# Later splits and later accumulations of the last product's weights in the gate stage of a transformer trunk kernel

## Chip, cores and metric

The kernel runs on one core of one Trainium2 chip. The metric is the device time of one execution in microseconds (us); a kernel's time is the median of its runs.

## The reference

One layer, in float32, of a trunk with sliding-window attention and a gated embedding (512 tokens, width 2048). Cut to what matters:

```python
hn = rmsnorm(x, norm_g)
y = swa_mixer(hn, swa_w_in, swa_w_out, swa_sinks, rel_bias)   # attention, times silu(gate), then @ w_out
x = x + y
emb = p @ ple_proj                                  # 512x256 @ 256x2048
g = jax.nn.sigmoid(rmsnorm(x, ple_norm) @ ple_gate) # 512x2048 @ 2048x2048
x = x + emb * g
return rmsnorm(x, final_g)
```

The change touches the product with `ple_gate`, which is called the gate stage here.

## The kernel before

**Precision.** Every product of two float32 matrices is made of three matmuls (`mm3`, lines 126 to 128). An operand is split into a high part (the value cast to fp32r, on ACT) and a low part (the value minus the high part, on DVE), and high x high, low x high and high x low are accumulated in PSUM. For the weights of the last two stages `_split` does this: line 754 is the cast (`bhi`), line 755 the subtraction (`blo`).

**Fewer products.** The 2048x2048 products with `w_out` and `ple_gate` are computed by blocks in Strassen's manner, with seven block products. Six of them are run one after the other in the order `ORDER_PLE = (1, 7, 6, 5, 3, 4)`; the remaining one, numbered 2, is broken up once more into small products that are spread over products 1, 7 and 6. Counted with it, the code's `p == 5` is the fifth product, `p == 3` the sixth and `p == 4` the last, and so they are called here.

**Pieces.** The weights come in pieces of 128x1024 (512 KB). `Pieces.specs` lists them in the order of use. A product has eight pieces, four for each half `jj`; between them stand pieces for the small products (half the matmuls) and for the embedding (`ple_proj`, the tile `e` in PSUM). A whole piece feeds 12 matmuls. `B.get(i)` hands out piece `i`. Before that it calls `ahead(i)`, which issues loads some pieces ahead (line 747, on SP's queue, into `braw`, whose buffers are reused in turn) and has the splits of pieces up to `i + 2` made.

**Grown pieces.** Products 7, 6 and 4 use weights that are sums of blocks, each being the one before plus one more block. So product 7's eight pieces are loaded into tiles called `grown` ("seed"), and POOL issues accumulating DMAs (line 734, `accum_op=ALU.add`) that add the next block on top of the same tile once it has been split: once for product 6, once more for product 4. `get(i)` puts the accumulation for the next product on the list `due` at position `i + 2` (behind a seed) or `i + 6`; it is issued when `get` reaches that position.

**The last product's weights.** The eight pieces of product 4 are split by `split_last(k)`, ahead of time, at places that the table `early` names by product, half and step: line 762 is the cast on ACT (tile `last`), line 763 the subtraction on DVE (tile `low`). Piece 0 is split in the fifth product, pieces 1 to 6 in the sixth, piece 7 behind it. The last product then runs as four blocks (tiles `last` and `open` in PSUM), between which the rows of the result are normalised and stored.

**Posts.** When a product's sums are complete, their values are passed through `gated`: sigmoid on ACT (line 1224), times the embedding on DVE (line 1226), added to `x1`, and squared on ACT for the final norm (line 1233). For eight of the sixteen parts the addition is an accumulating DMA that POOL issues (line 1228, `x1s<-s`); for the others it is on DVE (line 1230). Line 1392 and line 1267 are steps that sum products; line 855, 867 and 868 prepare and split the other operand for the next product; line 1243 and 1251 are of the final norm.

**Order.** In the gate stage the instructions of every engine (PE, SP, DVE, ACT and POOL) run in the order in which the program issues them. So a later place in the Python program is a later place in each engine's queue, and an instruction that waits holds up those behind it on its own engine.

Of the kernel before, what the change touches and what calls it, by code (L numbers as in the profile page):

```python
# [55 lines left out]
def trunk_kernel(ctx: ExitStack, tc: tile.TileContext, a: dict):  # L56
# [31 lines left out]
    class Weights:  # L88
# [24 lines left out]
        def get(self, i):  # L113
            while self.asked <= min(i + self.ahead, len(self.srcs) - 1):
                self.todo.append(partial_of(self._make, self.asked))
                self.asked += 1
            while self.todo and not (self.apart and i < len(self.made)):
                self.todo.pop(0)()
            return self.made[i]
# [281 lines left out]
    for b in range(exact, BUCKETS):  # L401
        d = np.nonzero(bk == b)[0]
        if len(d):
            lo, n = P - 1 + int(d.min()), len(d)
# [315 lines left out]
    class Pieces:  # L720
# [37 lines left out]
        def split_last(self, k, hi, lo):  # L758

            i = len(self.specs) - 8 + k  # L760
            raw = self.base.pop(i)
            nc.scalar.copy(hi, raw)
            nc.vector.tensor_sub(lo, raw, hi.bitcast(F32))
            self.made[i] = tuple([t[:, :512], t[:, 512:]] for t in (hi, lo))
# [14 lines left out]
        def get(self, i):  # L779
            self.ahead(i)  # L780

            key = self.specs[i][2]
            if key is not None:
                n = next((n for n in range(i + 1, len(self.specs)) if self.specs[n][2] == key), None)
                if n is not None:
                    self.due.append((i + (2 if self.specs[i][0] == "seed" else 6), n))
                    self.due.sort()
            while self.due and self.due[0][0] <= i:
                self._prepare(self.due.pop(0)[1])
            return self.made.pop(i)  # L790
# [494 lines left out]


    rooms4 = {}
    early = {(5, 0, 3): 0, (3, 0, 0): 1, (3, 0, 2): 2, (3, 1, 0): 3, (3, 1, 1): 4, (3, 1, 2): 5, (3, 1, 3): 6}

    def split_last(k):  # L1290
        if k % 2 == 0:
# [108 lines left out]
        next(g)  # L1400
    for g in two:
        next(g)
    split_last(7)
    for g in two:
        run(g)
# [50 lines left out]
    n = done[3]  # L1456
# [81 lines left out]
```

## Time and profile before

| | us |
|---|---|
| median of 3 runs | 791.35 (791.12 to 792.30) |
| the profiled execution | 791.86 |
| its span | 790.1 |
| PE busy | 780.4 |
| DVE busy | 605.9 |
| ACT busy | 505.8 |
| POOL busy | 138.4 |

In the profile, times are in us from the start of the span unless marked ns. PE is the tensor engine's matmuls and PEld its weight loads, DVE the vector engine, ACT the scalar engine, POOL the GpSimd engine, SP the engine whose queue issues the plain loads and stores. A row of the timeline has the start, the busy time, engine, line, operation, tiles written `<-` read, and in brackets the idle time of the engine before it with what ended that. A row of the stretches has the stretch, its length, then each engine's busy time with its count of instructions, the granted clock of PE as a share, the DMA share (the mean busy share of 16 DMA engines, which can read a little over 1) and GB/s. A row of the waits has who waited, for whom, the total in us, how often, and the longest.

### The profile page before, as it was taken

To read this page: it belongs to the slowest core of one execution; us is meant where nothing else is said; L and a number is where in the kernel's file an instruction comes from. 1 tells how busy PE (TensorE), PEld (TensorE's weight loads), DVE (VectorE), ACT (ScalarE), POOL (GpSimd) and SP (SyncE) were. 2 spreads that over 40 slices of the span, in tenths; PEclk is the share of its full clock that TensorE was granted. 3 is DMA by queue.
4 is the path that set the end of the run, shared out by engine and by line. 5 is a ranking of instruction groups with operands and counts; after the bars stand their busy time and mean duration, and the time that the engine had idled before them with its cause. 6 is when DMAs were issued, how large, how long until landed. Compare 5 with 4: busy or idle time off the path is not lost.

```text
span 790.1 us, 11098 instructions
## 1 busy us (share of the span) xinstructions
PE 780.4 (99%) x3726; PEld 652.1 (83%) x3726; DVE 605.9 (77%) x1036; ACT 505.8 (64%) x1066; POOL 138.4 (18%) x257
## 2 busy tenths in 40 slices
PE   9999999999999999999999999999999999999995
PEld 8888888888888888888888888888888888887885
DVE  4546697876877687777777899778869588978995
ACT  6643576666767586766666645456689676556943
POOL 0201423132223323122222200000000022201000
PEclk9999999999999999999999999999999999999998
DMA  9978889999999989999997498667873899979733
GB/s 344 285 215 296 191 251 316 299 278 270 277 268 262 268 236 316 238 300 263 279 272 185 133 364 317 224 206 237 267 265 107 299 291 250 252 229 250 213 108 106
DMA packets 47561, 198.07 MB, mean 251 GB/s; under 512 B 7104, under 2 KB 8128, under 8 KB 41744
## 3 DMA queue, kind: packets, MB, share of 16 engines
q1 hardware_dynamic: 38208, 150.91, 55.1%
q0 software_dynamic: 9296, 46.46, 30.4%
q8 instruction: 29, 0.48, 0.2%
q14 instruction: 28, 0.23, 0.1%
HBM read 189.16 MB, written 71.35 MB: 330 GB/s over the span
## 4 chain that ended last, share of the span: by engine, by line
PE 93%; DVE 3%; issue 2%; ACT 1%; POOL 0%; POOLq 0%; DVEq 0%; ACTq 0%
PE gps L126 7%; PE gps L127 7%; PE gps L128 7%; PE qps L126 7%; PE qps L127 7%; PE qps L128 7%; PE o L127 6%; PE o L126 6%; PE o L128 6%; PE g L127 4%; PE g L128 4%; PE g L126 4%; PE s L485 2%; PE vps L290 2%; PE pt L551 2%
## 5 line engine op out<-in xcount | busy, mean ns | idle before, releaser
L755 DVE TENSOR_TENSOR blo<-braw,bhi 128x1024 fp32r<-128x1024 f32 x108 | 131.3, 1221 | 37.0 <-ACT bhi L754 36.2
L754 ACT CAST bhi<-braw 128x1024 fp32r<-128x1024 f32 x108 | 113.4, 1051 | 57.9 <-PE o L128 20.7
L126 PE MATMUL gps<-xh,whi 128*128 128x512 f32 x256 | 100.0, 391 | 0.0
L127 PE MATMUL gps<-xl,whi 128*128 128x512 f32 x256 | 100.0, 390 | 0.0
L128 PE MATMUL gps<-xh,wlo 128*128 128x512 f32 x256 | 99.7, 390 | 0.0
L126 PE MATMUL qps<-xh,whi 128*128 128x512 f32 x224 | 87.8, 392 | 0.0
L127 PE MATMUL qps<-xl,whi 128*128 128x512 f32 x224 | 87.4, 390 | 0.0
L128 PE MATMUL qps<-xh,wlo 128*128 128x512 f32 x224 | 87.3, 390 | 0.0
L110 DVE TENSOR_TENSOR wlo<-wraw,whi 128x1024 fp32r<-128x1024 f32 x60 | 73.5, 1226 | 3.8 <-ACT whi L109 3.7
L570 POOL TENSOR_SCALAR_AFFINE_SELECT own<-r 64x512 fp32r<-64x512 f32 (+1 forms) x48 | 32.4, 675 | 244.9 <-DVE r L560 242.4
L127 PE MATMUL o<-blo,fho 128*128 128x512 f32 x192 | 74.9, 390 | 0.0
L126 PE MATMUL o<-bhi,fho 128*128 128x512 f32 x192 | 74.9, 390 | 0.0
L128 PE MATMUL o<-bhi,flo 128*128 128x512 f32 x192 | 74.8, 389 | 0.0
L556 ACT CAST r<-pt 128x256 fp32r<-128x256 f32 x64 | 23.9, 373 | 68.5 <-PE pt L551 68.1
L109 ACT CAST whi<-wraw 128x1024 fp32r<-128x1024 f32 x60 | 62.3, 1040 | 5.4 <-issue 4.1
L127 PE MATMUL g<-blo,fhg 128*128 128x512 f32 x160 | 62.5, 391 | 0.4 <-DVE blo L755 0.4
L126 PE MATMUL g<-bhi,fhg 128*128 128x512 f32 x160 | 62.8, 392 | 0.0
L128 PE MATMUL g<-bhi,flg 128*128 128x512 f32 x160 | 62.4, 390 | 0.0
L128 PEld LDWEIGHTS gps<-xh,wlo 128*128 128x128 f32 x256 | 48.1, 188 | 10.2
L126 PEld LDWEIGHTS gps<-xh,whi 128*128 128x128 f32 x256 | 48.1, 188 | 9.2
L529 ACT ACTIVATE t<-t,sm 128x129 f32<-128x129 f32 (+1 forms) x128 | 49.7, 390 | 8.9 <-DVE sm L525 7.3
L127 PEld LDWEIGHTS gps<-xl,whi 128*128 128x128 f32 x256 | 48.1, 188 | 8.8
(240 smaller groups left out, 1762.7 us busy)
## 6 DMA issues: line engine op xcount, KB each, us to landing
wraw<-in_w_gate_in SPq DMA_DIRECT2D x32, 512.0 KB, 8.1
w_out<-in_w_out POOLq DMA_DIRECT2D x32, 512.0 KB, 8.9
braw<-w_out SPq DMA_DIRECT2D x32, 512.0 KB, 4.7
wraw<-in_w_q SPq DMA_DIRECT2D x28, 512.0 KB, 6.8
braw<-in_w_out SPq DMA_DIRECT2D x22, 512.0 KB, 4.5
braw<-in_ple_gate SPq DMA_DIRECT2D x22, 512.0 KB, 5.3
xw<-in_first SPq DMA_DIRECT2D x14, 640.5 KB, 6.6
w_out<-in_w_out SPq DMA_DIRECT2D x16, 512.0 KB, 10.8
```

The lines of the kernel that those rows point to most:

```text
L109: nc.scalar.copy(hi, raw)
L110: nc.vector.tensor_sub(lo, raw, hi.bitcast(F32))
L126: nc.tensor.matmul(ps, sh, mh, start=first, stop=False, skip_group_check=more)
L127: nc.tensor.matmul(ps, sh, ml, start=False, stop=False, skip_group_check=more)
L128: nc.tensor.matmul(ps, sl, mh, start=False, stop=last, skip_group_check=more)
L290: nc.tensor.matmul(v_ps[t], h[:, c], part_of(high_at, 256, 512), start=f, stop=e, skip_group_check=True)
L485: nc.tensor.matmul(s_ps[:, u, : 2 * n], st, of_keys[:, first * 2 * QB : (first * QB + n) * 2], start=True, stop=True)
L529: nc.scalar.activation(su, su, AF.Exp, bias=sm[:, u : u + 1], accum_out=sm[:, 2 + u : 3 + u])
L556: nc.scalar.copy(rh, src)
L570: nc.gpsimd.affine_select(out=flat(own), in_=flat(r).bitcast(F32), pattern=[[0, 8], [sign, HB]], compare_op=ALU.is_ge, fill=0.0, base=-HB ...
L754: nc.scalar.copy(hi, raw)
L755: nc.vector.tensor_sub(lo, raw, hi.bitcast(F32))
```

## The change

Three edits: an accumulation for product 4 is put on the list 14 positions behind the piece instead of 6; the table `early` no longer has an entry in product 5, and the pieces move up by one in the entries of product 3; pieces 6 and 7 are both split behind product 3, where piece 7 alone was.

```diff
@@ Pieces.get
-                    self.due.append((i + (2 if self.specs[i][0] == "seed" else 6), n))
+                    self.due.append((i + (2 if self.specs[i][0] == "seed" else 14), n))
@@ gate stage
-    early = {(5, 0, 3): 0, (3, 0, 0): 1, (3, 0, 2): 2, (3, 1, 0): 3, (3, 1, 1): 4, (3, 1, 2): 5, (3, 1, 3): 6}
+    early = {(3, 0, 0): 0, (3, 0, 2): 1, (3, 1, 0): 2, (3, 1, 1): 3, (3, 1, 2): 4, (3, 1, 3): 5}
@@
     for g in two:
         next(g)
+    split_last(6)
     split_last(7)
     for g in two:
         run(g)
```

## The prediction

> **What bounds the kernel now.** I read the page first, then the waits of PE, then the timeline around the one wait found there.
>
> ```profile
> span 790.1 us, 11098 instructions
> PE 780.4 (99%) x3726; PEld 652.1 (83%) x3726; DVE 605.9 (77%) x1036; ACT 505.8 (64%) x1066; POOL 138.4 (18%) x257
> ...
> DMA  9978889999999989999997498667873899979733
> ...
> PE 93%; DVE 3%; issue 2%; ACT 1%; POOL 0%; POOLq 0%; DVEq 0%; ACTq 0%
> ```
>
> PE is busy for 99% of the span and carries 93% of the chain that ended last, so an edit of the weight splits gains only where it ends a wait of PE, and loses only where it makes one. A digit of the DMA line is one slice of 19.75 us: in the last quarter of the span, the gate stage, most digits but the last few are 7 to 9, so the transfers are the second resource to watch. From 620 to 782 us the view of waits lists this and nothing else for PE:
>
> ```profile
> PE g L127 <- DVE blo L755: 0.4, 1, 0.4
> ```
>
> The timeline of PE places it:
>
> ```profile
> 712.34 0.39 PE L126 MATMUL g<-bhi,fhg 128*128 128x512 f32 x1
> 713.15 0.50 PE L127 MATMUL g<-blo,fhg 128*128 128x512 f32 x1 [0.42 <-DVE blo L755]
> 713.49 0.40 PE L128 MATMUL g<-bhi,flg 128*128 128x512 f32 x1
> 713.73 0.40 PE L126 MATMUL g<-bhi,fhg 128*128 128x512 f32 x1
> ```
>
> Undisturbed ones of this shape follow each other like this:
>
> ```profile
> 743.05 0.39 PE L126 MATMUL g<-bhi,fhg 128*128 128x512 f32 x1
> 743.28 0.39 PE L127 MATMUL g<-blo,fhg 128*128 128x512 f32 x1
> 743.50 0.39 PE L128 MATMUL g<-bhi,flg 128*128 128x512 f32 x1
> ```
>
> That is a step of 0.227 us. At 712 the steps are 0.81, 0.34 and 0.24: 0.58 + 0.11 + 0.01 over the pitch, and with a few more 0.24 steps behind them about **0.76 us** lost. What DVE does just before:
>
> ```profile
> 709.61 1.21 DVE L855 TENSOR_TENSOR hT<-hT,hT 128x1024 f32<-128x1024 f32 x1
> 710.74 1.22 DVE L763 TENSOR_TENSOR low<-grown,last 128x1024 fp32r<-128x1024 f32 x1
> 711.88 3.49 DVE L755 TENSOR_TENSOR blo<-braw,bhi 128x1024 fp32r<-128x1024 f32 x3
> ```
>
> L763 is the split of the last product's piece 0, the one that the change takes out of the fifth product. The split that PE waits for (first of the three at 711.88) comes right behind it.
>
> **Part 1: piece 0's split leaves the fifth product.** DVE's steps from start to start are 1.14 us (710.74 to 711.88), more than PE's stall of 0.58. Without L763 the awaited split ends 1.14 us earlier and the stall goes: **-0.76 us**. What is late next: the casts of the sixth product, below.
>
> **Part 2: one more split behind the sixth product.** All splits between move up by one piece but keep their number in each slot, so DVE and ACT there are unchanged. Behind the sixth product stand two splits where one stood: one L763 more on DVE (1.14 us) and one cast on ACT.
>
> ```profile
> 758.56 1.22 DVE L763 TENSOR_TENSOR low<-grown,last 128x1024 fp32r<-128x1024 f32 x1
> ...
> 773.17 0.69 DVE L1392 TENSOR_TENSOR s<-last,s 128x512 f32<-128x512 f32 x1 [0.90 <-PE last L128]
> ...
> 777.30 0.69 DVE L1243 TENSOR_TENSOR x1s<-x1s,fg 128x512 f32<-128x512 f32 x1 [0.79 <-ACT s L1233]
> ...
> 781.79 0.42 DVE L1226 TENSOR_TENSOR s<-e,s 128x256 f32<-128x256 f32 x1 [1.53 <-PE e L128]
> ```
>
> DVE works without a gap from 758.56 to about 772; 1.14 us more uses up the 0.90 of idle time before 773.17, leaves 0.24, and the 1.53 before 781.79 takes that. When PE needs them:
>
> ```profile
> L127 PE MATMUL last<-low,fhg x24: 389/389/390, 754.2 to 772.5; 128*128 128x512 f32 x24
> ```
>
> The first block of the last product (24 matmuls and 6 of its embedding) and pieces 4 and 5 of the second (12) take 42 x 0.227 = 9.5 us, so piece 6 is due at about 763.7, and both splits end by about 761. Cost **0**, at most 1.14 if the cover fails.
>
> **Part 3: the accumulations.** POOL issues them in program order, and nothing ties POOL to PE's pace except what each of its DMAs waits for. So "14 pieces behind" changes only their order against the other POOL DMAs, the accumulations of `gated` into x1s (L1228), which wait for DVE. By the instruction order of the changed kernel, the accumulations for pieces 0 to 2 stay ahead of all of them; pieces 3 and 4 go behind the first two x1s DMAs, piece 5 behind the third, pieces 6 and 7 behind the sixth. Before:
>
> ```profile
> 673.31 0.86 POOL L734 DMA_DIRECT2D grown<-in_ple_gate  x1 [2.62 <-DVE blo L755]
> ...
> 688.49 0.86 POOL L734 DMA_DIRECT2D grown<-in_ple_gate  x1 [1.88 <-DVE blo L755]
> 709.65 1.76 POOL L1228 DMA_DIRECT2D x1s<-s  x2 [20.30 <-DVE s L1226]
> 719.46 0.86 POOL L1228 DMA_DIRECT2D x1s<-s  x1 [8.05 <-DVE s L1226]
> 722.52 0.89 POOL L1228 DMA_DIRECT2D x1s<-s  x1 [2.19 <-issue]
> 725.21 1.76 POOL L1228 DMA_DIRECT2D x1s<-s  x2 [1.80 <-DVE s L1226]
> 735.36 1.75 POOL L1228 DMA_DIRECT2D x1s<-s  x2 [8.40 <-DVE s L1226]
> ```
>
> Pieces 3 to 7 were issued at 673.31 to 688.49. They will go out at about 711 (two), 720 (one) and 727 (two). Piece 3's split takes the place that piece 4's had:
>
> ```profile
> 745.36 1.04 ACT L762 CAST last<-grown 128x1024 fp32r<-128x1024 f32 x1
> ```
>
> The others follow later, so the accumulations' lateness costs nothing by itself. What counts is where their traffic falls:
>
> ```profile
> 620.00:635.00 15.00, 15.00 (x67) 12.41 (x67) 9.15 (x9) 9.52 (x14) 1.29 (x2) 1.00 0.99 365
> 655.00:700.00 45.00, 45.00 (x200) 37.29 (x199) 35.83 (x40) 26.75 (x30) 8.62 (x10) 1.00 1.02 257
> 700.00:705.00 5.00, 5.00 (x24) 4.14 (x23) 5.00 (x8) 2.04 (x3) 0.00 (x0) 1.00 0.36 128
> 710.00:740.00 30.00, 29.58 (x131) 24.14 (x130) 25.98 (x30) 22.03 (x36) 6.67 (x8) 1.00 0.91 242
> ```
>
> The last two columns are the DMA share and GB/s. From 620 to 635 almost only plain loads run: 365 GB/s at 0.99, so a load of 0.524 MB takes 1.42 us of all 16 engines. From 655 to 700 the engines worked 45 x 1.02 = 45.9 us for 257 GB/s x 45 us = 11.6 MB, 22 transfers of 0.524 MB; with about half of them accumulations, 11 loads take 15.6 us and an accumulation (45.9 - 15.6) / 11 = **2.75 us** (2.5 to 3.0 for 12 or 10 of them). So 13.8 us of DMA work leaves a stretch that stood it without a PE wait and enters one that is 91% full: 710 to 740 has 30 x 0.09 = 2.7 us free.
>
> What is due there, by the sixth product's casts:
>
> ```profile
> 738.66 0.62 ACT L1233 ACTIVATE s<-x1s 128x512 f32<-128x512 f32 x1
> ...
> 740.40 2.00 ACT L754 CAST bhi<-braw 128x1024 fp32r<-128x1024 f32 x2
> ```
> ```profile
> 741.48 2.36 DVE L755 TENSOR_TENSOR blo<-braw,bhi 128x1024 fp32r<-128x1024 f32 x2 [0.26 <-ACT bhi L754]
> ```
>
> The cast at 740.40 is followed by its subtraction (741.48 to about 742.7), and PE takes that piece at 743.05 (row above): about 0.3 us of slack. The square at 738.66 on ACT, ahead of it in order, reads the x1s whose DMAs were issued at 725.21, and those now queue on POOL's queue behind pieces 3, 4 and 5. So by about 740 the DMA engines have to deliver, beyond what they delivered before: three accumulations, 8.25 us, and of piece 6's, which runs beside the loads then, half: 1.4 (between none and all of it). Sum 9.6 us. Against it stand: 2.7 us free; the pair of x1s issued at 735.36, which slips behind pieces 6 and 7 and is read last, by the squares at 759; and an earlier start.
>
> ```profile
> x1s<-s POOLq DMA_DIRECT2D x8, 256.0 KB, 5.5
> ```
> ```profile
> 692.14 1.05 ACT L754 CAST bhi<-braw 128x1024 fp32r<-128x1024 f32 x1 [1.67 <-PE g L128]
> ...
> 697.69 1.05 ACT L754 CAST bhi<-braw 128x1024 fp32r<-128x1024 f32 x1 [3.13 <-DMA braw<-ple_gate]
> ...
> 759.30 0.61 ACT L1233 ACTIVATE s<-x1s 128x512 f32<-128x512 f32 x1
> ```
>
> With 5.5 us from issue to landing, most of the slipping pair's work fell before 740; I estimate 2.3 us. The load behind 697.69 was late behind accumulations that now go later. The cast at 692.14 waits 1.67 us for PE anyway, so about 1.5 of the 3.13 are the transfer's, and loads and x1s of 700 to 712 start that much sooner, in the hole of 0.36 at 700. Supply 2.7 + 2.3 + 1.5 = 6.5 us. Short by 3.1, and with 0.3 of slack PE waits **about 2.8 to 3.1 us** in all between 725 and 750, mostly on blo behind late casts. I take 3.1, since a stall also slows the matmuls just behind it (0.11 above).
>
> From both sides: at 2.5 us per accumulation and nothing of piece 6 ahead of the loads, 7.5 - 6.5 - 0.3 = 0.7; with all five ahead of the loads and squares, 13.8 - 6.5 - 0.3 = 7.0.
>
> The Trainium skill, page "DMA: Bandwidth & Descriptors", section "Queues, rings and completion order", says that each DMA engine alternates between the queues that have work, a packet of several descriptors at a time. By that the loads would keep their turn beside piece 6, as the half above has it; served strictly in order of issue, all of piece 6 would come first and the stall would be 4.2. No row here shows the alternation.
>
> **Sum.** -0.76 + 0 + 3.1 = **+2.3 us**. The profiled execution took 791.86 us (span 790.1 and 1.76 around it) and would become 794.2; the median shown, 791.35, is 0.5 below it, and gives **793.7**.
>
> **Rivals.**
> (a) *The prefetch hides the moved traffic; not slower.* The place is the same stretch. Loads are issued four pieces ahead, when the buffer four pieces back is freed, and from 655 to 700 loads ran beside ten accumulations at a share of 1.02 with no PE wait. If the shortage at 740 is under 0.3 us, only part 1 is left: 791.35 - 0.76 = 790.6. Up to a shortage of 0.3 + 0.76 it is not slower; that is the case if an accumulation costs under 2.16 us there (3.5 x 2.16 - 6.5 = 1.06) or the early start is worth 3.5 us rather than 1.5. Against it: from 655 to 700 no x1s transfers ran beside them.
> (b) *An accumulation costs the engines no more than a load.* Then three and a half of 1.42 us are 5.0, under the supply of 6.5: also 790.6. The row for 655 to 700 speaks against it: 257 GB/s at a full share against 365. The Trainium skill, same page, section "Anatomy of one DMA — SWDGE (gpsimd) path", gives 2.0 us plus bytes at 436 GB/s, which would be an estimate of 1.2 us of movement for each of these, and by it the sum would be -0.76 too; the trace has 2.75.
> (c) *The end becomes DVE's.* The extra split pushes the chain behind 758.56 and the two idle times do not take it: up to +1.14 - 0.76 = +0.4, 791.7. It decides if over 0.90 + 1.53 us come on DVE behind 758; 1.14 do.
> (d) *The moved accumulations do nothing*, because POOL's order does not change. The order shows five of eight moving, so this is out as a whole, but for pieces 0 to 2 it holds.
>
> **How the numbers follow.** A measurement of this kernel can tell about 0.2%, 1.6 us, from no change: 789.8 to 792.9. The forecast's mechanism at a size beyond that has 0.64; (a), with a small rest of stall included, 0.23; (b) 0.06; (c) 0.04. A gain over 1.6 us has no row, since the one wait listed for PE from 620 to 782 is worth 0.76; 0.03 is left for what I have not seen. Faster 0.03, same 0.33, slower 0.64. The likeliest case alone spans 793 to 797; the range takes in (a) and (b) and ends near the upper bound, 791.35 + 7.0 - 0.76 = 797.6, cut at 797.
>
> **What would show it.** Right: no wait at the piece of 713; L734 issues between L1228 issues from 710 to 730; DMA share about 1.0 from 712 to 745; ACT casts (L754) or squares (L1233) that wait for DMAs of braw or x1s, and PE waits on blo L755 of some 3 us between 725 and 752; DVE still idle before the L1226 at 781.79 (shifted). Wrong: loads of braw that ACT does not wait for between 712 and 750, and no PE wait there (a), or a DMA share that stays under 1.0 with the accumulations in it (b).

## The result, and the profile after

The changed kernel takes **795.49 us** against 791.33 before (medians of 6 runs each); the ratio is 1.0051, 95% interval 1.0037 to 1.0064. Slower by 4.2 us: the forecast was +2.3 with a range of 790.5 to 797.0. One execution of the changed kernel, the one profiled first, ran at a granted clock of 0.85 and is left out of the ratio (the median of the other five is 795.36); the profile shown here is of the same kernel run again at 0.996 (medians 795.07 against 791.08, ratio 1.0055, 1.0042 to 1.0068). Its page begins:

```profile
span 794.7 us, 11096 instructions
PE 782.3 (98%) x3726; PEld 652.0 (82%) x3726; DVE 606.4 (76%) x1036; ACT 505.9 (64%) x1066; POOL 139.2 (18%) x257
...
DMA  9988899999999989999997589667863999479823
```

The same 3726 matmuls run. Of the 4.6 us by which the span grew, 2.7 are idle time of PE, and 1.9 stand in its busy time (782.3 against 780.4): a matmul at a stall takes 0.50, as below, where others take 0.39. PE's waits over the whole run, but for one at the start of the program:

```profile
PE open L126 <- ACT open L1373: 1.2, 1, 1.2
PE e L127 <- DVE blo L755: 1.0, 2, 0.8
...
PE g L127 <- DVE blo L755: 0.8, 1, 0.8
```

The wait at 713 is gone. Others have come, for weights (`blo`) in the sixth product, and one in the last product, for a bank that ACT opens. In PE's timeline:

```profile
723.30 0.50 PE L126 MATMUL e<-bhi,pTh 128*128 128x512 f32 x1
724.56 0.50 PE L127 MATMUL e<-blo,pTh 128*128 128x512 f32 x1 [0.76 <-DVE blo L755]
724.90 0.40 PE L128 MATMUL e<-bhi,pTl 128*128 128x512 f32 x1
...
737.12 0.50 PE L127 MATMUL g<-blo,fhg 128*128 128x512 f32 x1 [0.83 <-DVE blo L755]
...
777.19 0.39 PE L128 MATMUL e<-bhi,pTl 128*128 128x512 f32 x1
778.76 0.39 PE L126 MATMUL open<-last,fhg 128*128 128x256 f32 x1 [1.19 <-ACT open L1373]
```

The step to 724.56 is 1.26 us where 0.227 is the pitch (the usual step from start to start), so a wait listed with 0.76 costs 1.03. Marks on PE's timeline give the account. From the piece of 712 to the first matmul of the last product: 41.59 us before, 44.73 after. From there to the last matmul: 27.47 before, 28.92 after. So **+3.14 and +1.45, together 4.6**, the difference of the spans (794.7 - 790.1). The medians differ by 4.0: the profiled execution took 796.38 us, 1.3 above the median of 795.07.

POOL's queue, as foreseen (seven of its rows; x2 is two DMAs in a row):

```profile
708.13 1.76 POOL L1228 DMA_DIRECT2D x1s<-s  x2 [37.49 <-DVE s L1226]
709.26 2.42 POOL L734 DMA_DIRECT2D grown<-in_ple_gate  x2
719.07 0.86 POOL L1228 DMA_DIRECT2D x1s<-s  x1 [7.39 <-issue]
719.62 1.21 POOL L734 DMA_DIRECT2D grown<-in_ple_gate  x1
725.66 0.86 POOL L1228 DMA_DIRECT2D x1s<-s  x1 [4.83 <-issue]
728.33 1.78 POOL L1228 DMA_DIRECT2D x1s<-s  x2 [1.81 <-DVE s L1226]
729.48 2.44 POOL L734 DMA_DIRECT2D grown<-in_ple_gate  x2
```

And the stretches (the last two columns are the DMA share and GB/s):

```profile
655.00:700.00 45.00, 45.00 (x200) 37.28 (x199) 37.29 (x42) 26.76 (x30) 4.30 (x5) 1.00 0.76 202
...
710.00:740.00 30.00, 28.35 (x120) 21.84 (x118) 20.92 (x26) 19.36 (x30) 9.64 (x11) 1.00 1.05 263
740.00:750.00 10.00, 10.00 (x44) 8.02 (x44) 7.28 (x9) 7.26 (x12) 0.00 (x0) 1.00 1.06 301
```

From 655 to 700 the share fell from 1.02 to 0.76: 45 x 0.26 = 11.7 us of DMA work left it, 2.3 us for each of the five accumulations. The stretch from 710 to 740 went from 0.91 to 1.05. The casts of weights feel it:

```profile
722.20 1.05 ACT L754 CAST bhi<-braw 128x1024 fp32r<-128x1024 f32 x1 [4.20 <-DMA braw<-in_ple_proj]
...
745.98 1.05 ACT L754 CAST bhi<-braw 128x1024 fp32r<-128x1024 f32 x1 [1.94 <-DMA braw<-in_ple_gate]
```

Issued from 709 to 718.5, the DMAs took (issue to landing, median):

```profile
braw<-in_ple_gate SPq DMA_DIRECT2D x3, 512.0 KB, 11.3
grown<-in_ple_gate POOLq DMA_DIRECT2D x2, 512.0 KB, 10.9
braw<-in_ple_proj SPq DMA_DIRECT2D x1, 512.0 KB, 11.6
```

The same three weight loads before:

```profile
braw<-in_ple_gate SPq DMA_DIRECT2D x3, 512.0 KB, 6.0
```

### The profile page after: what moved, and what is told of

The parts are those of the page before. It is cut to its first block, busy times and chain, and to the rows that moved or that the text cites. A ratio compares the mean times of both kernels' runs of the same rounds, so it can differ in the third digit from the quotient of the medians.

```text
span 865.8 us, 11096 instructions
## 1 busy us (share of the span) xinstructions
PE 856.5 (99%) x3726; PEld 671.7 (78%) x3726; DVE 612.1 (71%) x1036; ACT 506.3 (58%) x1066; POOL 138.0 (16%) x257
## 5 line engine op out<-in xcount | busy, mean ns | idle before, releaser
L128 PE MATMUL gps<-xh,wlo 128*128 128x512 f32 x256 | 106.7, 417 | 0.0
L126 PE MATMUL gps<-xh,whi 128*128 128x512 f32 x256 | 106.7, 417 | 0.0
L127 PE MATMUL gps<-xl,whi 128*128 128x512 f32 x256 | 106.7, 417 | 0.0
L127 PE MATMUL qps<-xl,whi 128*128 128x512 f32 x224 | 93.5, 417 | 0.0
L128 PE MATMUL qps<-xh,wlo 128*128 128x512 f32 x224 | 93.5, 417 | 0.0
L126 PE MATMUL qps<-xh,whi 128*128 128x512 f32 x224 | 93.4, 417 | 0.0
L126 PE MATMUL o<-bhi,fho 128*128 128x512 f32 x192 | 80.2, 418 | 0.0
L127 PE MATMUL o<-blo,fho 128*128 128x512 f32 x192 | 80.1, 417 | 0.0
L128 PE MATMUL o<-bhi,flo 128*128 128x512 f32 x192 | 79.9, 416 | 0.0
L560 DVE TENSOR_TENSOR r<-pt,r 128x256 fp32r<-128x256 f32 x56 | 23.8, 425 | 66.5 <-ACT r L556 66.4
```

What stands on the lines that cost most here:

```text
L126: nc.tensor.matmul(ps, sh, mh, start=first, stop=False, skip_group_check=more)
L127: nc.tensor.matmul(ps, sh, ml, start=False, stop=False, skip_group_check=more)
L128: nc.tensor.matmul(ps, sl, mh, start=False, stop=last, skip_group_check=more)
L560: nc.vector.tensor_sub(rl, src, rh.bitcast(F32))
```

## The experiments

Theory A is the one of the prediction: the moved accumulations crowd the transfers, weights come late, PE waits. Theories B, C, D, T and A' are given where they are tested. "Before" in a ratio is the kernel before, run beside the other on the same chip.

**The change again.** No edit.

> The changed kernel once more, for a profile at the full granted clock. Theory A (the moved accumulations crowd the transfers of 710 to 750 us, and PE waits for late weights): 795 us; PE's waits in the gate stage sum to 4 to 5 us, on blo L755 behind ACT casts that wait for DMAs of braw or for x1s; the wait at 713 us is gone. Rival B (the second split behind the sixth product pushes the DVE chain of the tail): no new PE waits before 755 us, and the stretch from the last product's first matmul to the end is some 4 us longer than before (36 us there).

795.07 us, the profile above. A's waits are there, and the wait at 713 is gone; the listed waits sum to 3.0 us, not to the 4 to 5 expected, while 4.6 are lost by PE's marks. B is right about one of the four waits, the one in the last product, and that stretch is 1.45 us longer, not 4.

**Only the splits.**

```diff
-                    self.due.append((i + (2 if self.specs[i][0] == "seed" else 14), n))
+                    self.due.append((i + (2 if self.specs[i][0] == "seed" else 6), n))
```

(against the changed kernel, as are all the diffs below unless said otherwise)

> Only the splits are moved; the accumulations stay 6 pieces behind. Theory A: the DMA traffic is as before, the wait at 713 us goes, -0.76 us: 790.6 (ratio 0.999). Rival B: slower by 4 to 5 us, 795 to 796, as with the whole change.

790.45 against 791.08, ratio 0.9996 (0.9987 to 1.0004). Once more, beside other kernels:

> Only the splits moved, once more, beside the two above: 0.5 to 0.8 us under before, 790.4, if the gain of the wait at 713 us is real; the same as before if the earlier difference was spread between runs.

790.95 against 791.23, ratio 0.9994 (0.9985 to 1.0003). The gain of 0.3 to 0.6 us stays inside what the runs can tell. In the profiles it is plain: in both, the warm-up at the start is PE's only wait; of the first:

```profile
PE warm_ps L141 <- PEq L1529: 0.9, 1, 0.9
```

and the stretch from the piece of 712 to the last product took 40.80 us, 0.79 less than before (predicted 0.76). B falls: two splits behind the sixth product cost nothing by themselves.

**Only the accumulations** (against the kernel before).

```diff
-                    self.due.append((i + (2 if self.specs[i][0] == "seed" else 6), n))
+                    self.due.append((i + (2 if self.specs[i][0] == "seed" else 14), n))
```

> Only the accumulations are moved (14 pieces behind); the splits stand where they stood. Theory A: the whole loss and not the gain of the splits, 795.5 to 797. Also piece 0's split sits in the fifth product again, so the wait near 713 us stays. Rival B: as before, 791.3.

794.38, ratio 1.0040 (1.0027 to 1.0054): the loss comes with the accumulations, a little less than expected. PE's waits in the sixth product are those of the whole change, and the one in the last product is missing:

```profile
PE e L127 <- DVE blo L755: 0.8, 1, 0.8
PE g L127 <- DVE blo L755: 0.6, 1, 0.6
```

The miss in the expectation: the wait at 713 went here too. The load that ACT waited for at 697.69 is no longer late (ACT lists no wait for a DMA from 694 to 713), and piece 0's split on DVE starts 1.86 us earlier than at 710.74. Against PE it is 1.46, since PE reaches the same piece 0.40 us earlier in this run (711.94 against 712.34):

```profile
708.88 1.22 DVE L763 TENSOR_TENSOR low<-grown,last 128x1024 fp32r<-128x1024 f32 x1
```

So that wait needed both, the late load and the split, and either edit ends it.

**Fewer accumulations moved.** 10, 8 and 7 pieces behind instead of 14, which puts three, two and one of them behind the first two x1s DMAs, back to back.

```diff
-                    self.due.append((i + (2 if self.specs[i][0] == "seed" else 14), n))
+                    self.due.append((i + (2 if self.specs[i][0] == "seed" else 10), n))   # 8, 7
```

> The whole change with the accumulations 10 pieces behind: by the instruction order pieces 5 to 7 go behind the first two x1s DMAs, pieces 3 and 4 stay ahead of them. Theory A: three moved instead of five, 8.25 us of DMA work instead of 13.8 into the crowded stretch, all three issued at about 711 us, where transfers have some time free: 791 to 793.5. Rival B: 795 to 796, as the splits are those of the whole change. Rival C (not the amount but the x1s transfers that queue behind accumulations on POOL's queue cost, through the squares on ACT): the three x1s DMAs of 719 to 726 us queue behind all three, so at least as slow as the whole change.

> The whole change with the accumulations 8 pieces behind: pieces 6 and 7 go behind the first two x1s DMAs, back to back as in the whole change. Theory A: the loads issued at about 710 us land behind both (5.5 us) as in the whole change, so the first stall near 724 us of about 1.2 us is there, but nothing follows from 730 on: 791.3 to 792.2. Rival D (only the total of 13.8 us over the whole stretch counts): 5.5 us are taken by the free time, no stall, 790.5.

> The whole change with the accumulations 7 pieces behind: only piece 7's goes behind the first two x1s DMAs. Theory A: one accumulation, 2.75 us, delays the load issued at about 710 us by less than its slack: no stall, 790.5 (ratio 0.999). If any accumulation behind the x1s DMAs costs: 792 or more.

| moved, how | time, us | ratio (interval) | three loads behind, us to landing | piece of 712 to last product, us |
|---|---|---|---|---|
| none (only the splits) | 790.45 | 0.9996 (0.9987 to 1.0004) | 4.7 | 40.80 |
| one | 791.45 | 1.0005 (0.9996 to 1.0014) | 8.0 | 40.88 |
| two in a row | 792.11 | 1.0015 (1.0005 to 1.0024) | 10.7 | 42.29 |
| three in a row | 794.58 | 1.0047 (1.0034 to 1.0059) | 13.5 | 44.92 |
| five: 2, 1, 2 (the change) | 795.07 | 1.0055 (1.0042 to 1.0068) | 11.3 | 44.73 |

The loads are the three plain weight loads issued from about 711 to 718 us, with the median of one profile each. The expectation for three was a miss: 791 to 793.5 was expected, 794.58 measured. By the last column three in a row cost 4.1 us against only the splits, and the five of the change 3.9: the number of moved accumulations does not decide. (The whole change is still slower in all, by what it loses in the last product.)

The times to landing vary between profiles: with only the splits they were 4.7 and, run again, 5.7; with one accumulation ahead 8.0 and, in the last two runs below, 6.9 and 6.5; with two 10.7, 11.3 and, in the run with only the accumulations, 10.8; with three 13.5. By the means each accumulation ahead adds about 2.8 us; single steps are too uncertain to read. The Trainium skill, page "DMA: Bandwidth & Descriptors", section "Anatomy of one DMA — SWDGE (gpsimd) path", has bytes at 436 GB/s, an estimate of 1.2 us; the trace does not agree for accumulations, at 2.3 us of the DMA engines by the stretches and 2.8 us of delay.

With one, ACT waits for the load and PE does not; with two, PE waits once:

```profile
721.65 1.06 ACT L754 CAST bhi<-braw 128x1024 fp32r<-128x1024 f32 x1 [1.72 <-DMA braw<-in_ple_gate]
```
```profile
723.25 1.05 ACT L754 CAST bhi<-braw 128x1024 fp32r<-128x1024 f32 x1 [2.64 <-DMA braw<-in_ple_gate]
```
```profile
735.37 0.50 PE L127 MATMUL g<-blo,fhg 128*128 128x512 f32 x1 [0.57 <-DVE blo L755]
```

(the first row is of one moved, the others of two). The place was a miss: with two the wait near 724 is absent and comes at 735, where ACT has had no idle time since 730.74 and DVE none since 732.95. D (the total of 5.5 us fits into the free time) falls, and so does C: with three in a row, as in the whole change, no profile lists an ACT wait for x1s DMAs in the gate stage, and every wait of ACT for a DMA there is for braw. With three, in PE's waits:

```profile
PE g L127 <- DVE blo L755: 1.7, 3, 0.8
...
PE e L127 <- DVE blo L755: 0.8, 1, 0.8
```

**Plain transfers.**

```diff
-                nc.gpsimd.dma_start(t, src, accum_op=ALU.add)
+                if i >= len(self.specs) - 5:
+                    nc.gpsimd.dma_start(t, src)
+                else:
+                    nc.gpsimd.dma_start(t, src, accum_op=ALU.add)
```

> The whole change, but the five moved accumulations are plain transfers of the same blocks into the same tiles from the same queue (pieces 3 to 7 then hold one block instead of the sum). Theory A with the price that the profile gave (2.75 us of the DMA engines for an accumulation, 1.42 for a plain transfer): 7.1 us of work moved instead of 13.8, and a load behind two of them is 2.7 us less late; most of the stall goes, 790.6 to 792. If the cause is that transfers of any kind stand ahead of the loads, or their order on POOL's queue: 794 to 795, as with accumulations.

791.37, ratio 1.0007 (0.9998 to 1.0016). This kernel leaves out the additions of pieces 3 to 7. Same queue, same order, same number, and PE has no wait in the sixth product (40.82 us from the piece of 712 to the last product); the three loads land in 6.7 us. So what the accumulations cost above plain transfers is the cause, not their place in POOL's queue. What is left is in the last product, 0.73 us longer than with only the splits (28.20 against 27.47):

```profile
773.48 0.38 PE L126 MATMUL open<-last,fhg 128*128 128x256 f32 x1 [0.48 <-ACT open L1376]
```

**The tail** (against only the splits).

```diff
             nc.vector.tensor_sub(lo, raw, hi.bitcast(F32))
+            if k == 7:
+                nc.vector.tensor_sub(lo, raw, hi.bitcast(F32))
```

> Only the splits are moved (accumulations 6 pieces behind), and piece 7's subtraction behind the sixth product is done twice: 1.14 us more of DVE there. Theory T (the tail's DVE work stands some 0.75 us ahead of what PE's last block needs, so a DVE that is over 0.75 us later than PE makes PE wait for the bank that ACT opens): PE waits about 0.4 us on ACT open L1373, 790.9. Without such a limit: 790.45, no wait in the tail.

791.36, ratio 1.0006 (0.9997 to 1.0015); this time alone does not show a cost, the trace does. PE takes the bank 0.41 us after the matmul ahead of it, 0.18 over the pitch, too short for the list of waits:

```profile
773.32 0.39 PE L128 MATMUL e<-bhi,pTl 128*128 128x512 f32 x1
773.73 0.38 PE L126 MATMUL open<-last,fhg 128*128 128x256 f32 x1
```

ACT's opening of it ran from 773.31 to 773.68, so PE does start when the bank opens, as T says; the step is 0.18 and the whole last product 0.28 us longer (27.75 against 27.47), where about 0.4 was expected.

**Accumulations one by one.** The same two or three as above, each behind another x1s DMA.

```diff
-                    self.due.append((i + (2 if self.specs[i][0] == "seed" else 14), n))
+                    self.due.append((i + (2 if self.specs[i][0] == "seed" else {5: 10, 6: 12, 7: 13}.get(n - len(self.specs) + 8, 6)), n))
```

(for two: `{6: 8, 7: 11}`)

> The splits of the whole change, and three accumulations moved as with 10 pieces behind, but one by one: piece 5's behind the first two x1s DMAs, piece 6's behind the third, piece 7's behind the sixth. Theory A' (what stalls PE is a burst: a load issued behind a run of accumulations lands after all of them, and PE stalls once that exceeds the loads' slack of about 3 us): no load stands behind more than one, 790.5 to 791.8. Theory A as predicted (the total of DMA work over the stretch counts): as with three in one run, 794 to 795.

> Two accumulations moved as with 8 pieces behind (792.1), but one by one: piece 6's behind the first two x1s DMAs, piece 7's behind the third. Theory A': no wait of PE in the sixth product, 790.5 to 791.4. Theory A (total): 792, as with the two in one run.

Three apart: **791.76**, ratio 1.0007 (0.9998 to 1.0016), where three in a row took 794.58. Two apart: 790.97, ratio 0.9996 (0.9987 to 1.0005), where two in a row took 792.11. No wait of PE in the sixth product in either. With three apart, what was issued from 709 to 718.5:

```profile
braw<-in_ple_gate SPq DMA_DIRECT2D x3, 512.0 KB, 6.5
...
grown<-in_ple_gate POOLq DMA_DIRECT2D x1, 512.0 KB, 8.4
```

From the piece of 712 to the last product they take 40.86 and 40.80 us, as with only the splits (40.80); with three, the last product is 0.41 us longer. So A', that a burst stalls PE, holds with both times inside what it expected, and the total over the stretch does not count: the same transfers are nearly free there, if no load stands behind two of them. In both runs the accumulations go out 7 to 10 us apart; the runs do not tell how much closer they may stand.

## Why the prediction was right, and where its steps were off

**Part 1 held**, and the early start of part 3 too. The wait at 713 went; 0.79 us in the trace of the splits alone against 0.76. The work of 709 came 1.46 us sooner against PE by the accumulations alone, against 1.5. Within the whole change part 1 adds nothing, since moving the accumulations ends the same wait.

**Part 3 held in direction and place, and its account of it failed.** The sign, the stretch (724 to 755), the waits of ACT on braw and of PE on blo, the share of 1.05 and the order on POOL's queue are as written. The size: 3.1 us of waits were forecast; against the splits alone (40.80 us) the stretch took 44.73, so 3.9. But the step "short by 3.1", a balance of DMA work against free time up to 740, is not what happens. Three moved one by one and three in a row put the same work into the stretch, with 2.8 us between their times and 4.1 between their stretches (40.86 and 44.92). What decides is how much stands shortly ahead of a weight load. When ACT waited 1.72 us for a load, PE lost nothing; at 2.64 it lost 1.5 us, later on; at 4.20 it stalled at once. An estimate from these rows: the loads have some 2 to 3 us of slack, one accumulation takes about 2.8 or less, and two in a row exceed it. That the balance came out near the truth was luck: the change happens to issue in pairs. It also put the first wait near 740; it came at 724, behind the first pair.

The price in that balance was too high as well. It took half of the transfers from 655 to 700 as accumulations, 2.75 us for each; with 12 or 10 of them the same sum gives 2.6 to 2.9, not 2.5 to 3.0. The changed profile gives 2.3 by what left the stretch (with three in a row the share there is 0.88, which gives 2.1). With 2.3 the balance would be short by 3.5 x 2.3 - 6.5 = 1.6 us only, so a price that was too high made up for part of what the balance does not hold. Its 0.3 us of slack is read to the matmul at 743.05, which takes `bhi`; the one that takes `blo` starts at 743.28, so the slack there is about 0.6.

**The halved accumulation of piece 6** stood on loads taking turns with accumulations. With two in a row, for DMAs issued from 709 to 718.5:

```profile
grown<-in_ple_gate POOLq DMA_DIRECT2D x2, 512.0 KB, 12.3
...
braw<-in_ple_proj SPq DMA_DIRECT2D x1, 512.0 KB, 8.9
```

The proj load went out just behind the pair, at 710.61, and landed at 719.5, ahead of both accumulations (720.5 and 724.4), so the queues do interleave. The Trainium skill, page "DMA: Bandwidth & Descriptors", section "Queues, rings and completion order", has the engines alternate between queues; this row agrees. But the next load landed at 723.2, between the two, and the two behind it after both: taking turns does not keep a run of accumulations from making the loads late.

**Part 2 was mis-sized: 0 forecast, 1.45 in the profile, and only together with part 3.** By the medians the whole change is 0.7 us above the accumulations alone (795.07 and 794.38), so 1.45, from an execution 1.3 us above its median, may be more than usual. The prediction looked for the cover at DVE's idle 0.90 before 773 and 1.53 before 781. The limit is earlier: the bank of the last block, which ACT opens behind a square that DVE feeds. With the splits alone:

```profile
772.28 0.37 ACT L1373 ACTIVATE open<-s 128x256 f32<-128x256 f32 x1
773.46 0.28 PE L126 MATMUL open<-last,fhg 128*128 128x256 f32 x1
```

So 773.46 - 772.28 - 0.37 = 0.8 us are spare. In the changed kernel the late loads put DVE 6.1 us behind that run while PE was 4.0 behind it (first matmul of the last product: 757.01 against 753.06). There DVE had work from 764.10 up to the square with one gap of 0.25 us, and the idle time before the last L1226, 1.53 in the kernel before, was down to 0.32:

```profile
764.10 2.54 DVE L763 TENSOR_TENSOR low<-grown,last 128x1024 fp32r<-128x1024 f32 x2
...
786.32 0.42 DVE L1226 TENSOR_TENSOR s<-e,s 128x256 f32<-128x256 f32 x1 [0.32 <-PE e L128]
```

The square and the opening behind it on ACT:

```profile
777.71 0.63 ACT L1233 ACTIVATE s<-x1s 128x512 f32<-128x512 f32 x1 [1.80 <-DVE x1s L1230]
...
778.34 0.37 ACT L1373 ACTIVATE open<-s 128x256 f32<-128x256 f32 x1
```

6.1 - 4.0 - 0.8 = 1.3, close to the 1.34 by which the step from 777.19 to 778.76 exceeds the pitch. The same sum, of the starts of `low` behind the sixth product and of the last product's first matmul against the splits alone, gives 0.6 for the plain transfers (758.82 and 752.45) and 0.3 for three accumulations one by one (759.50 and 753.45), where the last product is 0.73 and 0.41 us longer. For three in a row (761.36 and 756.66) DVE is less behind than PE, and the last product is not longer (27.48). Rival (c) saw this stretch but looked at its wrong end. That the extra split on DVE is the cause is shown by the accumulations alone, where one split fewer stood there and the last product took 27.61 us, and by the doubled subtraction.

**Rivals (a) and (b)** fall for the change as it is: the prefetch did not hide it, and an accumulation does cost more than a load (2.3 us of the DMA engines by the stretches against the prediction's 1.42; and with two ahead the loads land after some 10.9 us, with two plain transfers ahead after 6.7). (a) describes the kernels with single accumulations. **(d)** held for pieces 0 to 2, as said there.

**What stays open.** One moved accumulation measured 791.45, above the 790.5 expected, without any PE wait in the gate stage of its profile; whether it costs anything is inside the intervals. The best of all versions is the splits alone, 790.45 and 790.95; that it beats the kernel before is shown in PE's waits and not by its interval.

## What to carry to other kernels

When a transfer is moved to a later place, ask which load is issued right behind it and by how much that load is ahead of its use; count the moved transfers that stand in one run ahead of it, not their share of a whole stretch. An accumulating DMA counts for more than a plain one of its bytes, here about 1.6 times (2.3 us against 1.42). And where a vector engine is full to the end of a kernel, lateness given to it early is not won back unless the engine it feeds is as late (as with three in a row): look for the first point in the tail that waits for it, not the last.

## What the runs showed of the hardware that was not expected

Each accumulating DMA of 512 KB into SBUF that stands ahead delays the loads behind it by about 2.8 us on average (about 5.2 us to landing behind none, 13.5 behind three), where with two plain ones ahead from the same queue they landed after 6.7 us. A wait of PE costs more than its idle time: at 724.56 the listed 0.76 is 1.03 by the steps from start to start, and the next step is 0.34 instead of 0.227.
